# Products of one width together in the gate, up, B, C, x, q and k projections of a hybrid decoder layer

## The chip, the cores and the metric

The kernel runs on one core of one Trainium2 chip. The metric is the device time of one execution in microseconds; the time before is the median of three runs. A profile is one further execution, recorded by the hardware profiler. TensorE (PE) does the matmuls, ScalarE (ACT) and VectorE (DVE) do elementwise work, GpSimd (POOL) and SyncE (SP) mostly start transfers.

## The reference, cut to what matters

One decoder layer on 256 tokens of 1024 channels, all in float32: a gated feed-forward, a mixer with two branches in parallel, and a second gated feed-forward.

```python
h = h + 0.5 * rmsnorm(swiglu(rmsnorm(h, ffn1_pre_g), w_gate, w_up, w_down), ffn1_post_g)
u = rmsnorm(h, mix_pre_g)
z, xbc, dt_raw, q, k, v, gate_logits = split(u @ w_in)
y_ssd = ssd_branch(z, xbc, dt_raw, ...)      # convolution over xbc = (x, B, C), chunked state space
y_att = diff_attn_branch(q, k, v, ...)       # differential attention
h = h + rmsnorm((g0 * y_ssd + g1 * y_att) @ w_out, mix_post_g)
h = h + 0.5 * rmsnorm(swiglu(...), ffn2_post_g)
```

The projections in question are `x @ w_gate` and `x @ w_up` (1024 by 2816 each, in both feed-forwards), and the parts of `u @ w_in` that make B, C, x, q and k.

## The kernel before, in words

Each float32 operand of a projection is split into two parts of the matmul's reduced type: hi is the rounded value, lo is what is left. A product is the sum of three: weight hi by activation hi, weight hi by activation lo, weight lo by activation hi. The activations u lie as [128, 4, 2, 256] tiles, hi beside lo, so that one matmul of 512 columns does both products with a weight's hi part ("wide"), and one of 256 columns does the product with its lo part ("narrow").

Weights come in chunks of 1 MB, loaded by SyncE into three raw buffers (`load_to`, L232). `split_steps` (L244) makes hi by a ScalarE cast (whi, L259) and lo by a VectorE subtraction (wlo, L260), each in two halves. `take` (L306) keeps three chunks split ahead.

`mm_w` (L335) is one call: a chunk of 1024 by 256 weights, so two blocks of 128 outputs (half 0 and half 1). Each half has a PSUM bank of 512 columns. Half 0 does its 8 wide products and then its 8 narrow ones; half 1 does 8 narrow and then 8 wide. Each half is evicted when it is done: ScalarE copies the right 256 columns of the bank (L348, or L351 with a scale), and VectorE adds the left 256 to them (L349, L352). Both halves' banks come from `pj` (L81), a pool of three banks in turn. Another pool of five banks, `bg` (L89), serves transposes, scores and other background products.

Who calls it: the feed-forward loop (`ffn`, L881 to L898), gate and then up for each of nine chunks; C and B (L1203 to L1209, named pbc); x (L1489 to L1495, pxs); q and k in turn (L1510 to L1518, pq and pk), with a scale for q. Between x and q stands z (L1498 to L1504, pz), whose products are all narrow (`mm_t`) and whose bank ScalarE copies out (sz, L1503).

Beside these projections runs background work that Python generators hand out in steps (`Background`, L1461): each `back.run(us)` adds to what is due, and steps are emitted until their stated costs have used it up. During x it is `cb_work` (L1214): C times B for each group (pcb). During z, q and k it is `ssd_work` (L1227): transposes of x (px, L1233), the decay tiles E (made from a broadcast load acb by ScalarE and VectorE, L1249 to L1255; named by group, half and pair, such as E211), and the products py of E and X (L1265). Then `ssd_norm` (L1276, pn). In the attention and gates stage it is `att_work`.

Between L830 and L1523, so for most of both feed-forwards' gate and up calls and from C and B to the last k, the order of instructions on each engine is not the program's: the framework's scheduler places them by dependencies, priority and its own costs when the kernel is built. Each engine then runs its own list in that order. Elsewhere TensorE follows the program (`own_order`). The SiLU of z and its two changes of the activation table (L1505 to L1508) stand between z and q.

Of the kernel before, what the change touches and what calls it, by code (L numbers as in the profile page):

```python
# [18 lines left out]
AF = mybir.ActivationFunctionType  # L19
ALU = mybir.AluOpType  # L20
# [6 lines left out]
P = 128  # L27
T = 256
D = 1024
FF = 2816  # L30
KD = D // P
# [23 lines left out]
def tile_hybrid_layer(ctx: ExitStack, tc: tile.TileContext, x, ffn1_pre_g, ffn1_w_gate, ffn1_w_up,  # L55
# [4 lines left out]
    nc = tc.nc  # L60
# [5 lines left out]
    def k4(shape, name, dt=F32):  # L66
        return sb.tile(shape, dt, tag="k4", name=name, bufs=K4_BUFS)
# [4 lines left out]
    def k2(shape, name, dt=F32):  # L72
        return sb.tile(shape, dt, tag="k2", name=name, bufs=K2_BUFS)
# [7 lines left out]
    def pj(name):  # L81

        return ps.tile([P, 512], F32, tag="pj", name=name, bufs=3)
# [5 lines left out]
    def bg(shape, name):  # L89
        return ps.tile(shape, F32, tag="bg", name=name, bufs=5)  # L90
# [197 lines left out]
    def split_to(n):  # L288

        while len(splits) < min(n, len(units)):  # L290
            of, p = units[len(splits)]
            if p is not None:
                splits.append(of.split(p))
                continue
            for _ in split_steps():
                pass

    def ahead_of(i, n):

        n *= 4  # L300
        while n > 0 and i < len(units):
            n -= 4 if units[i][1] is None else 1
            i += 1
        return i

    def take(ahead=AHEAD):  # L306

        i = taken[0]
        taken[0] += 1
        split_to(ahead_of(i, ahead))  # L310
        (of, p), w = units[i], splits[i]
        splits[i] = None
        if p is not None:
            return w
        his, los = w
        nj = chunks[of][1][1] // 2
        return (lambda j: his[j // nj][:, j % nj, :], lambda j: los[j // nj][:, j % nj, :])
# [14 lines left out]
            for j in ks:  # L332
                nc.tensor.matmul(acc[m], wl(j)[:, cs], ah(k0 + j), start=False, stop=last and j == ks[-1])

    def mm_w(dst, name, w, act, scale=None):  # L335


        (wh, wl), (ah, _, ahl) = w, act
        for m in range(2):
            acc = pj(f"{name}{m}")  # L340
            cs = slice(m * P, (m + 1) * P)
            hi = [(acc, wh(j), ahl(j)) for j in range(KD)]
            lo = [(acc[:, :T], wl(j), ah(j)) for j in range(KD)]
            terms = lo + hi if m else hi + lo
            for i, (to, w_, x_) in enumerate(terms):
                nc.tensor.matmul(to, w_[:, cs], x_, start=i == 0, stop=i == len(terms) - 1, skip_group_check=m == 1)  # L346
            if scale is None:
                nc.scalar.copy(dst[:, m, :], acc[:, T:])  # L348
                nc.vector.tensor_tensor(dst[:, m, :], acc[:, :T], dst[:, m, :], ALU.add)  # L349
            else:  # L350
                nc.scalar.activation(dst[:, m, :], acc[:, T:], AF.Copy, scale=scale)  # L351
                nc.vector.scalar_tensor_tensor(dst[:, m, :], acc[:, :T], scale, dst[:, m, :], ALU.mult, ALU.add)  # L352

    def mm_nat(acc, w, act, k0, first, last, late):

# [32 lines left out]
    def act_table(name):  # L388
        f = nc.scalar.preload_act_table_set(name)
        for prev in act_since:  # L390
            tc.add_manual_dep(f.ins, prev, order, reason="activation table")
        act_since.clear()
        act_fence[0] = f.ins.name

    def act(*args, **kw):
        a = nc.scalar.activation(*args, **kw)
        if act_fence[0] is not None:
            tc.add_manual_dep(a.ins, act_fence[0], order, reason="activation table")
        act_since.append(a.ins.name)
        act_last[0] = a.ins  # L400
# [65 lines left out]
    for name, v in (("mx", mix_pre_g), ("f2", ffn2_pre_g),  # L466
                    ("ng", ssd_norm_g), ("cb", ssd_conv_b), ("sg", da_subln_g)):
        n = v.shape[1] // P
# [7 lines left out]
    def new_u(tag):  # L476
        for i in range(2):
            uT[i] = sb.tile([P, 4, 2, T], F32R, tag="u8", name=f"u{i}_{tag}", bufs=2)

    act_u = (lambda j: uT[j // 4][:, j % 4, 0, :], lambda j: uT[j // 4][:, j % 4, 1, :],  # L480
             lambda j: uT[j // 4][:, j % 4, :, :])
# [146 lines left out]
    def load_gain(v, name):  # L628
        pg = k4([P, D], name)
        nc.gpsimd.dma_start(pg, v[0].partition_broadcast(P))  # L630
        return pg
# [220 lines left out]
    def ffn(post_v, tag, ready, turned, then, products):  # L852
        gu = []

        gh = k4([P, 4, T], f"gh_{tag}0", F32R)
        gl = k4([P, 4, T], f"gl_{tag}0", F32R)
        gu += [(gh[:, m, :], gl[:, m, :]) for m in range(4)]
        sgs = []

        def evict(b, i, acc, r):  # L860
            if i == 0:
                sgs.append(k2([P, 512], f"sg_{tag}b{b}"))
                act(sgs[b], acc, AF.Silu, scale=1.0 if r is None else r)
            elif r is None:
                nc.vector.tensor_tensor(sgs[b], acc, sgs[b], ALU.mult)
            else:
                nc.vector.scalar_tensor_tensor(sgs[b], acc, r, sgs[b], ALU.mult, ALU.mult)

        def back(b):
            bs = slice(b * P, (b + 1) * P)  # L870
            pt_ = bg([P, 4, P], f"pt_{tag}{b}")
            for m in range(4):
                nc.tensor.transpose(pt_[:, m, :], sgs[b][:, m * P:(m + 1) * P], ident)
            split(gh[:, :, bs], gl[:, :, bs], pt_)

        products(evict, back)
        back(1)
        del sgs
        then()
        sums = {}  # L880
        for j in range(2, FF // T):  # L881
            if j % 2 == 0:
                gh = k4([P, 4, T], f"gh_{tag}{j}", F32R)
                gl = k4([P, 4, T], f"gl_{tag}{j}", F32R)
            o = (j % 2) * 2
            gu += [(gh[:, o + m, :], gl[:, o + m, :]) for m in range(2)]
            sg = k2([P, 2, T], f"sg_{tag}{j}")
            mm_w(sg, f"pg_{tag}{j}", take(), act_u)
            act(sg, sg, AF.Silu)
            su = k2([P, 2, T], f"su_{tag}{j}")  # L890
            mm_w(su, f"pup_{tag}{j}", take(), act_u)
            nc.vector.tensor_tensor(sg, su, sg, ALU.mult)  # L892
            split(gh[:, o:o + 2, :], gl[:, o:o + 2, :], sg)
            if j // 2 in QUADS[tag]:
                if j % 2:
                    sums[j // 2] = sums_of(j // 2, even, sg)
                else:
                    even = sg  # L898
        act_table(EXP_LN)
        acc, rest, combine, pairs = mm_quads(gu, sums, tag)  # L900
        pg = load_gain(post_v, f"pg_{tag}")

        norms = [{}, {}]

        quarters = (slice(0, 256), slice(256, 512)) if tag == "f2" else ()
        tail = [pj(f"tail{i}")[:, :256] for i in range(len(quarters))]

        def half(b, q):
            parts = quarters if b == 1 and q == 1 and quarters else (slice(0, 512),)
            r = rest[b][q]  # L910
            for cs in parts:
                behind(nc.vector.tensor_tensor(r[:, cs], acc[b][q][:, cs], r[:, cs], ALU.add), "lo")
            if len(parts) > 1:
                norm_quarters(norms[b], b, q, r, pg, 4.0, tag, parts, tail)
            else:
                norm_half(norms[b], b, q, r, pg, 4.0, tag)

        def done(b):
            norm_end(norms[b], b, 4.0, tag)
            ready(b)  # L920

        mm_n(acc, gu, done, turned, pairs=pairs, begin=False,
             taken_all=combine, norms=norms, half=half, quarters=quarters, tail=tail)
# [199 lines left out]
    for jj in range(2):  # L1123
        for a in (uh, ul):
            for i in range(4):
                k = i * 2 + jj
                nc.tensor.matmul(pdt[i * H_SSD:(i + 1) * H_SSD, :], wdt[:, k, :], a(k).bitcast(F32),
                                 start=jj == 0 and a is uh, stop=jj == 1 and a is ul)
# [73 lines left out]
    cT = k4([P, 4, T], "cT")  # L1202
    for i in range(4):  # L1203
        acc = k2([P, 2, T], f"bc{i}")
        mm_w(acc, f"pbc{i}", take(), act_u)
        dst = (bT, cT)[i // 2]
        conv(acc, 16 + 2 * i, dst[:, (i % 2) * 2:(i % 2) * 2 + 2, :])
        if i == 1:
            cumulated()  # L1209
# [108 lines left out]
    qT = [None] * 2  # L1318
    kT = [None] * 2
# [167 lines left out]
    back = Background()  # L1487
    back.add(cb_work())
    for g in range(4):  # L1489
        xs[g] = k4([P, 4, T], f"xs{g}")  # L1490
        for i in range(2):
            acc = k2([P, 2, T], f"xr{g}{i}")
            mm_w(acc, f"pxs{g}{i}", take(), act_u)
            conv(acc, g * 4 + i * 2, xs[g][:, i * 2:i * 2 + 2, :])
            back.run(0.4)  # L1495
    act_table(EXP_LN)
    back.add(ssd_work(range(4)))
    for g in range(4):  # L1498
        sz[g] = k4([P, 4, T], f"sz{g}")
        for i in range(2):  # L1500
            acc = pjt(f"pz{g}{i}")
# [8 lines left out]
    for c in range(4):  # L1510
        if c % 2 == 0:
            qT[c // 2] = k4([P, 4, T], f"q{c}")
            kT[c // 2] = k4([P, 4, T], f"k{c}")
        o = (c % 2) * 2
        mm_w(qT[c // 2][:, o:o + 2, :], f"pq{c}", take(), act_u, 0.125)
        back.run(QK_US)
        mm_w(kT[c // 2][:, o:o + 2, :], f"pk{c}", take(), act_u)
        back.run(QK_US)  # L1518

    back.add(att_work())  # L1520
# [80 lines left out]
    acc = [[bg([P, 512], f"acc_mx{b}{q}") for q in range(2)] for b in range(2)]  # L1601
# [50 lines left out]
```

## Time and profile before

| | |
|---|---|
| median of 3 runs | 730.47 us (730.29 to 732.0) |
| the profiled execution, and its span in the trace | 730.56 us, 728.9 us |
| granted TensorE clock, mean | 0.999 of full speed |
| DVE busy | 607.5 us, 83% of the span |
| first q to the end of the last k | 339.08 to 390.95 us |
| PE, DVE, ACT busy in that stretch | 51.87, 44.94, 39.10 us |

A row of the timeline has the start in microseconds from the span's start, the time the row covers, the engine, the line, the operation, the tile written and those read (buffer numbers left out), the shapes and the count. In brackets stands the idle time just before it, and what ended it. Matmuls overlap in the pipeline, so the spacing of starts is their cost, and a single one lasts longer than its spacing.

### The profile page before, as it was taken

The numbers are of one execution on the slowest core, as the hardware profiler recorded it, in microseconds if no ns is written. First come the engines' busy times: TensorE is split into PE (matmuls) and PEld (weight loads), VectorE is DVE, ScalarE is ACT, GpSimd is POOL, SyncE is SP. The second block draws the span as 40 slices with busy tenths as digits, with TensorE's granted clock in tenths as the row PEclk, the third lists the DMA queues.
The fourth block names the chain that finished last, engine by engine and source line by source line (L and its number), as shares of the span: only waits on it lengthen the run. The fifth ranks groups of instructions, "written<-read, shape, count | busy, mean of one in ns | idle before, by whom it ended". The sixth has DMA issues, their size and how long they took to land.

```text
span 728.9 us, 10550 instructions
## 1 busy us (share of the span) xinstructions
PE 721.7 (99%) x4025; PEld 620.8 (85%) x4025; DVE 607.5 (83%) x933; ACT 472.8 (65%) x804; POOL 30.9 (4%) x63
## 2 busy tenths in 40 slices
PE   9999999999999999999999999999999999999996
PEld 8888888888878889999888788888888888888885
DVE  6978788999979999777996997785784878789996
ACT  5657566667767676869965577782663757566562
POOL 4300000000200000000000000000010000000000
PEclk9999999999999999999999999999999999999999
DMA  8874645567664557665564664465461654654551
GB/s 299 233 262 147 226 161 186 174 223 268 195 217 123 170 172 248 212 205 176 164 222 148 210 209 147 142 244 190 125 237 43 232 187 161 230 197 150 176 199 58
DMA packets 94450, 137.92 MB, mean 189 GB/s; under 512 B 2668, under 2 KB 68800, under 8 KB 94400
## 3 DMA queue, kind: packets, MB, share of 16 engines
q1 hardware_dynamic: 91728, 129.51, 53.6%
q0 software_dynamic: 2368, 7.22, 3.3%
q8 instruction: 31, 0.51, 0.3%
q10 hardware_dynamic: 304, 0.53, 0.2%
q14 instruction: 19, 0.16, 0.1%
HBM read 136.17 MB, written 1.08 MB: 188 GB/s over the span
## 4 chain that ended last, share of the span: by engine, by line
PE 99%; DVE 0%; DVEq 0%; ACT 0%; issue 0%; ACTq 0%
PE pg_f L346 14%; PE pup_f L346 14%; PE pxs L346 6%; PE pws L363 6%; PE pgt L363 6%; PE acc_f2p L736 5%; PE acc_f1p L736 5%; PE pbc L346 3%; PE pk L346 3%; PE pq L346 3%; PE pn_f L379 3%; PE acc_mx L657 3%; PE pn_mx L363 3%; PE pn_f L363 3%; PE pwd L363 3%; PE acc_f1p L657 2%
## 5 line engine op out<-in xcount | busy, mean ns | idle before, releaser
L260 DVE TENSOR_TENSOR wlo<-raw,whi 128x1024 fp32r<-128x1024 f32 x216 | 257.5, 1219 | 19.0 <-ACT whi L259 17.8
L259 ACT CAST whi<-raw 128x1024 fp32r<-128x1024 f32 x216 | 219.4, 1050 | 14.1 <-DMA raw<-in_w_in_dram 3.5
L346 PE MATMUL pg_f<-u_f,whi 128*128 128x512 f32 x288 | 72.4, 392 | 0.0
L346 PE MATMUL pup_f<-u_f,whi 128*128 128x512 f32 x288 | 71.6, 391 | 0.0
L346 PEld LDWEIGHTS pup_f<-u_f,whi 128*128 128x128 f32 x288 | 52.9, 188 | 10.2
L346 PEld LDWEIGHTS pg_f<-u_f,whi 128*128 128x128 f32 x288 | 52.8, 188 | 10.1
L130 ACT CAST wqh<-wt 128x1024 fp32r<-128x1024 f32 x24 | 25.3, 1054 | 22.0 <-DVE wt L122 21.9
L346 PEld LDWEIGHTS pup_f<-u_f,wlo 128*128 128x128 f32 x288 | 37.1, 191 | 1.9 <-issue 0.3
L346 PEld LDWEIGHTS pg_f<-u_f,wlo 128*128 128x128 f32 x288 | 36.9, 191 | 1.4
L346 PE MATMUL pup_f<-u_f,wlo 128*128 128x256 f32 x288 | 37.8, 283 | 0.0
L346 PE MATMUL pg_f<-u_f,wlo 128*128 128x256 f32 x288 | 37.3, 283 | 0.0
L348 ACT COPY su_f<-pup_f 128x256 f32<-128x256 f32 x36 | 13.3, 370 | 36.7 <-PE pup_f L346 36.7
L349 DVE TENSOR_TENSOR su_f<-pup_f,su_f 128x256 f32<-128x256 f32 x36 | 15.1, 420 | 24.6 <-ACT su_f L348 24.6
L363 PE MATMUL pgt<-whi,u_mx 128*128 128x512 f32 x128 | 33.1, 393 | 0.0
L346 PE MATMUL pxs<-u_mx,whi 128*128 128x512 f32 x128 | 31.8, 394 | 0.0
L330 PE MATMUL pz<-u_mx,whi 128*128 128x256 f32 x128 | 31.6, 284 | 0.0
L331 PE MATMUL pz<-u_mx,whi 128*128 128x256 f32 x128 | 31.5, 284 | 0.0
L136 DVE TENSOR_TENSOR wql<-wt,wqh 128x1024 fp32r<-128x1024 f32 x24 | 29.1, 1219 | 0.2
L363 PEld LDWEIGHTS pgt<-whi,u_mx 128*128 128x128 f32 x128 | 23.6, 188 | 5.3 <-issue 0.7
L346 PEld LDWEIGHTS pxs<-u_mx,whi 128*128 128x128 f32 x128 | 23.2, 188 | 4.3
L320 ACT CAST gh_f<-sg_f 128x512 fp32r<-128x512 f32 x18 | 11.2, 620 | 23.3 <-DVE sg_f L892 23.3
L136 DVE TENSOR_TENSOR wql<-raw,wqh 128x1024 fp32r<-128x1024 f32 x18 | 21.8, 1219 | 4.4 <-ACT wqh L130 4.4
(415 smaller groups left out, 1585.7 us busy)
## 6 DMA issues: line engine op xcount, KB each, us to landing
raw<-in_w_in_dram SPq DMA_DIRECT2D x40, 1024.0 KB, 5.2
raw<-in_ffn_w_down_dram SPq DMA_DIRECT2D x22, 1024.0 KB, 4.8
raw<-in_ffn_w_gate_dram SPq DMA_DIRECT2D x20, 1024.0 KB, 5.4
raw<-in_ffn_w_up_dram SPq DMA_DIRECT2D x20, 1024.0 KB, 5.2
raw<-in_ssd_w_branch_dram SPq DMA_DIRECT2D x8, 1024.0 KB, 5.0
acb<-acd POOLq DMA_DIRECT2D x8, 512.0 KB, 4.4
raw<-in_da_w_branch_dram SPq DMA_DIRECT2D x4, 1024.0 KB, 5.0
raw<-in_w_out_dram SPq DMA_DIRECT2D x4, 1024.0 KB, 5.1
```

The source lines that it names most:

```text
L130: nc.scalar.copy(hi, src)
L136: nc.vector.tensor_sub(lo, src, hi.bitcast(F32))
L259: last_cast[0] = behind(nc.scalar.copy(hi, r[:, js, :]), "cast").ins
L260: m = nc.vector.tensor_sub(lo, r[:, js, :], hi.bitcast(F32))
L330: nc.tensor.matmul(acc[m], wh(j)[:, cs], ah(k0 + j), start=first and j == ks[0], stop=False)
L331: nc.tensor.matmul(acc[m], wh(j)[:, cs], al(k0 + j), start=False, stop=False)
L346: nc.tensor.matmul(to, w_[:, cs], x_, start=i == 0, stop=i == len(terms) - 1, skip_group_check=m == 1)
L349: nc.vector.tensor_tensor(dst[:, m, :], acc[:, :T], dst[:, m, :], ALU.add)
L363: nc.tensor.matmul(acc, a(k0 + j), b(j), start=first and i == 0, stop=last and i == 11)
L379: nc.tensor.matmul(accs[b], x_(k0 + j), w_(j), start=first and j == 0 and w_ is wh and x_ is acts[b][0], stop=last and j == 3 and w_ is wl)
L657: nc.tensor.matmul(acc[b][q][:, cs] if to is None else to, x_[:, ts], w_(kt)[:, halves[q]][:, cs], start=to is not None and kt == 0 and x_ ...
L736: nc.tensor.matmul(bank[p], x_, w_, start=p not in begun, stop=last and p in (1, 5, 6, 7))
```

## The change

`mm_w` becomes `mm_runs`. A call takes the products of one width for both halves together: an even call (n = 0) does half 0 wide, half 1 wide, half 0 narrow, half 1 narrow; an odd call (n = 1) does both narrow parts and then both wide parts. Each half is evicted after its second part, with the same two instructions as before. An odd call takes its two banks from the pool of five, unless `wide` is False; q and k pass False and are all odd. Gate is even and up odd; the four calls of B and C and the two of each x group alternate. In x the background is run after the even call alone, so C times B stands between a call that ends narrow and one that begins narrow.

```diff
+    def mm_part(acc, w, act, m, part, first):
+        (wh, wl), (ah, _, ahl) = w, act
+        to, w_, x_ = (acc, wh, ahl) if part == "hi" else (acc[:, :T], wl, ah)
+        for j in range(KD):
+            nc.tensor.matmul(to, w_(j)[:, m * P:(m + 1) * P], x_(j), start=first and j == 0,
+                             stop=not first and j == KD - 1, skip_group_check=True)
+    PARTS = (("hi", "lo"), ("lo", "hi"))
+    def mm_runs(dst, name, w, act, n, wide=True, scale=None):
+        banks = [bg([P, 512], f"{name}{m}") if n % 2 and wide else pj(f"{name}{m}") for m in range(2)]
+        for part in PARTS[n % 2]:
+            for m, acc in enumerate(banks):
+                mm_part(acc, w, act, m, part, part == PARTS[n % 2][0])
+                if part == PARTS[n % 2][1]:
+                    taken_from(acc, dst[:, m, :], scale)
...
-            mm_w(sg, f"pg_{tag}{j}", take(), act_u)
+            mm_runs(sg, f"pg_{tag}{j}", take(), act_u, 0)
...
-            mm_w(su, f"pup_{tag}{j}", take(), act_u)
+            mm_runs(su, f"pup_{tag}{j}", take(), act_u, 1)
...
-        mm_w(acc, f"pbc{i}", take(), act_u)
+        mm_runs(acc, f"pbc{i}", take(), act_u, i)
...
-            mm_w(acc, f"pxs{g}{i}", take(), act_u)
+            mm_runs(acc, f"pxs{g}{i}", take(), act_u, i)
             conv(acc, g * 4 + i * 2, xs[g][:, i * 2:i * 2 + 2, :])
-            back.run(0.4)
+            if i == 0:
+                back.run(0.4)
...
-        mm_w(qT[c // 2][:, o:o + 2, :], f"pq{c}", take(), act_u, 0.125)
+        mm_runs(qT[c // 2][:, o:o + 2, :], f"pq{c}", take(), act_u, 1, False, 0.125)
         back.run(QK_US)
-        mm_w(kT[c // 2][:, o:o + 2, :], f"pk{c}", take(), act_u)
+        mm_runs(kT[c // 2][:, o:o + 2, :], f"pk{c}", take(), act_u, 1, False)
```

`taken_from(acc, dst, scale)` is the copy and the add of L347 to L352, unchanged.

More of the change, by code (lines that the diff above doesn't have):

```diff
@@ L333, in mm_t, with taken_from @@
                 nc.tensor.matmul(acc[m], wl(j)[:, cs], ah(k0 + j), start=False, stop=last and j == ks[-1])
-    def mm_w(dst, name, w, act, scale=None):
+    def mm_part(acc, w, act, m, part, first):
         (wh, wl), (ah, _, ahl) = w, act
[L339 to L352, printed above, removed]
+        to, w_, x_ = (acc, wh, ahl) if part == "hi" else (acc[:, :T], wl, ah)
+        for j in range(KD):
+            nc.tensor.matmul(to, w_(j)[:, m * P:(m + 1) * P], x_(j), start=first and j == 0,
+                             stop=not first and j == KD - 1, skip_group_check=True)
+    def taken_from(acc, dst, scale=None):
+        if scale is None:
+            nc.scalar.copy(dst, acc[:, T:])
+            nc.vector.tensor_tensor(dst, acc[:, :T], dst, ALU.add)
+        else:
+            nc.scalar.activation(dst, acc[:, T:], AF.Copy, scale=scale)
+            nc.vector.scalar_tensor_tensor(dst, acc[:, :T], scale, dst, ALU.mult, ALU.add)
+    PARTS = (("hi", "lo"), ("lo", "hi"))
[6 more added lines that the diff above has]
+                    taken_from(acc, dst[:, m, :], scale)
     def mm_nat(acc, w, act, k0, first, last, late):
```

## The prediction

> **What bounds the kernel now.** I read first the page's busy table and its chain, then TensorE's timeline in the stages that the change touches, then ScalarE's and VectorE's timelines beside it.
>
> ```profile
> PE 721.7 (99%) x4025; PEld 620.8 (85%) x4025; DVE 607.5 (83%) x933; ACT 472.8 (65%) x804; POOL 30.9 (4%) x63
> ...
> PE 99%; DVE 0%; DVEq 0%; ACT 0%; issue 0%; ACTq 0%
> ```
>
> TensorE is busy for 99% of the span and carries 99% of the chain that ended last. So a gain has to come out of the matmuls' own spacing, and any wait that the change puts in front of a matmul is paid in full: there is no slack to hide it.
>
> In the timeline below a row's first number is the start of its first matmul, so the difference of two starts is what a row costs. "whi" rows are wide (512 columns), "wlo" rows narrow (256).
>
> ```profile
> 103.72 1.98 PE L346 MATMUL pup_f<-u_f,whi 128*128 128x512 f32 x8
> 105.53 2.08 PE L346 MATMUL pup_f<-u_f,wlo 128*128 128x256 f32 x16
> 107.44 2.00 PE L346 MATMUL pup_f<-u_f,whi 128*128 128x512 f32 x8
> 109.28 1.98 PE L346 MATMUL pg_f<-u_f,whi 128*128 128x512 f32 x8
> 111.09 2.08 PE L346 MATMUL pg_f<-u_f,wlo 128*128 128x256 f32 x16
> ```
>
> Eight wide behind wide cost 1.81 us (103.72 to 105.53, and 109.28 to 111.09), 0.227 each; eight wide behind narrow cost 1.84 (107.44 to 109.28). Sixteen narrow cost 1.91, 0.12 each. So a step from narrow to wide costs 0.03 us, and that is all that the change can take out of a call.
>
> **The change, part by part.** I compared the order in which the build places each kernel's instructions on the engines (there are no times in it). The matmuls are the same 3864; their neighbours differ. Steps from narrow to wide: 63 before, 38 after. They fall by 10 in each gated feed-forward (nine pairs of calls, and one pair of down products that no longer stands inside a call), by 2 in B and C, by 4 in x; in q and k they rise by 1 in sum, because there the build doesn't keep the groups together (below). Returns from plain fp32 work (transposes, py, C times B) to wide: 41 before, 35 after; to narrow: 5 before, 9 after.
>
> ```profile
> 340.92 1.95 PE L346 MATMUL pq<-u_mx,wlo 128*128 128x256 f32 x15
> 342.80 2.82 PE L1265 MATMUL py<-E,X 128*64 128x256 f32 x32
> 345.55 0.39 PE L346 MATMUL pq<-u_mx,wlo 128*128 128x256 f32 x1
> 345.78 2.00 PE L346 MATMUL pq<-u_mx,whi 128*128 128x512 f32 x8
> 347.61 1.03 PE L1233 MATMUL px<-ident,xs 128*128 128x128 f32 x8
> 348.40 2.07 PE L346 MATMUL pk<-u_mx,whi 128*128 128x512 f32 x8
> 350.31 2.08 PE L346 MATMUL pk<-u_mx,wlo 128*128 128x256 f32 x16
> ...
> 354.07 1.98 PE L346 MATMUL pq<-u_mx,whi 128*128 128x512 f32 x8
> ...
> 364.15 2.82 PE L1265 MATMUL py<-E,X 128*64 128x256 f32 x32
> 366.90 1.43 PE L346 MATMUL pk<-u_mx,whi 128*128 128x512 f32 x5
> 368.16 2.00 PE L346 MATMUL pq<-u_mx,whi 128*128 128x512 f32 x8
> ```
>
> *Savings.* 25 steps fewer at 0.03, less up to 0.01 each (a fresh narrow run of 16 takes 1.91, where 16 steps of 0.12 make 1.92): 25 x 0.025 = 0.6 us, between 0.5 and 0.75. Wide behind fp32: five take 1.26 (366.90 to 368.16) for 1.13, so 0.13 more; narrow behind fp32: one takes 0.23 (345.55 to 345.78) for 0.12, so 0.11 more. 6 x 0.13 - 4 x 0.11 = 0.35. Together 0.95 us, of which 0.6 lie ahead of the first q. Nothing runs over them, since TensorE is the chain itself.
>
> [...]
>
> *Evictions and banks.* Before, half 0 of a call is done 16 matmuls ahead of the call's end; now 8. In the feed-forwards, C, B and x this hides: odd calls take two of the five other banks, so a bank is written again only a whole call (5.6 us) or more after its half is done. The split weights cover too: by the build's order a call that begins narrow needs its low parts 1.8 us sooner, but they stand ready, three chunks ahead. I put both at nothing; if the cover failed it would be a wait of at most an eviction, under 1 us, at the start of a feed-forward.
>
> q and k are another matter: all their calls take the three pj banks, and each call now takes two at its start. Half 1 of a call needs the bank of half 0 of the call ahead, which was done 1.8 + 0.96 = 2.8 us earlier (eight wide, eight narrow), where before it had 5.6. An eviction is a ScalarE copy and then a VectorE add, each in its queue's place.
>
> ```profile
> 333.52 0.59 ACT L1503 COPY sz<-pz 128x512 f32<-128x512 f32 x1 [0.34 <-PE pz L333]
> ...
> 339.28 0.59 ACT L1503 COPY sz<-pz 128x512 f32<-128x512 f32 x1
> 339.76 1.28 ACT L396 ACTIVATE E<-acb,acs 128x128 f32<-128x128 f32 x4
> ...
> 348.08 1.05 ACT L259 CAST whi<-raw 128x1024 fp32r<-128x1024 f32 x1
> 349.04 0.65 ACT L351 ACTIVATE q<-pq 128x256 f32<-128x256 f32 x2
> 349.57 2.00 ACT L259 CAST whi<-raw 128x1024 fp32r<-128x1024 f32 x2
> 351.47 0.37 ACT L348 COPY k<-pk 128x256 f32<-128x256 f32 x1
> ...
> 355.79 1.28 ACT L396 ACTIVATE E<-acb,acs 128x128 f32<-128x128 f32 x4
> 356.98 0.62 ACT L396 ACTIVATE E<-E 128x512 f32<-128x512 f32 x1
> 357.50 1.27 ACT L396 ACTIVATE E<-acb,acs 128x128 f32<-128x128 f32 x4
> ```
>
> ```profile
> 349.17 1.23 DVE L260 TENSOR_TENSOR wlo<-raw,whi 128x1024 fp32r<-128x1024 f32 x1
> 350.31 0.75 DVE L352 SCALAR_TENSOR_TENSOR q<-pq,q 128x256 f32<-128x256 f32 x2
> ```
>
> Today the first q's half 0 is copied at 349.04 and added at 350.31 to 350.7, some 8 us after its last product; half 1 of k starts after the first eight of the narrow row at 350.31, so at 351.27. It gets by with about half a microsecond.
>
> In the changed order ScalarE does this: copy of z30, E blocks 200, 201, 210, one weight cast, copy of z31, one cast, E211, table, four SiLU, table, two casts, then q. Before, E200 and most of E201 stood ahead of z30's copy, and three of four casts ahead of z31's. So ScalarE now waits for z30's products with work behind it. Step by step on the clock of before: z30's copy at 333.52 - 0.6 = 332.9; 0.48 for it (339.76 less 339.28, rounded), three E blocks at 1.71 (355.79 to 357.50), a cast at 0.95 (two in 349.57 to 351.47): z31's copy at 339.45. From there to q's copy it was 349.04 - 339.28 = 9.76, now two casts more, 11.66: 351.1. VectorE must first split the two chunks' halves, 1.14 each (349.17 to 350.31), the first from the cast's end at 350.15: they end at 352.45, and the add of q's half 0 at 352.85.
>
> TensorE: first q at 339.08 - 0.6 = 338.48 (339.08 is 340.92 less eight wide behind narrow); 16 narrow 1.92, 15 wide 3.43, py 2.83, one wide 0.33, px 0.79, k's eight narrow 1.07, its eight wide 1.84: 350.7. Here it waits for the bank until 352.85: **2.15 us**. Eight narrow and eight wide more: k ends at 355.65 (354.07 before).
>
> Next, k's half 1 is copied right behind half 0 in ScalarE's queue, so ScalarE idles until 355.8; behind it are queued a cast, three E blocks, a cast and the copy of the second q: 0.3 + 0.95 + 5.13 + 0.95 puts that cast's end at 363.15, its VectorE split at 364.3, the add at 364.65. TensorE: second q 5.6, eight narrow and eight wide of the second k, 364.05: it waits **0.65 us**. From the third q on ScalarE has room and the waits end. That the build puts five wide products into the second q between its narrow halves, not eight, fits a first k that ended late.
>
> [...]
>
> Sum: 2.8 - 0.95 = +1.85 us. The profiled execution took 730.56 us (span 728.9), the median of the runs is 730.47; the forecast is 730.47 + 1.85 = **732.3**. Bounds: the first wait is between 0 (ScalarE at its old time, 349.04, and the two casts elsewhere) and 3.5 (z31's copy a further E block late); the second between 0 and 1.5.
>
> **Rivals.** *1. No wait, only the savings.* For: no row of TensorE in q and k shows a wait today, and the first of the two margins was kept. Against: two casts and three E blocks move behind a copy that waits for products. It would give 729.5.
> *2. Slower by more.* One mechanism: ScalarE reaches the first q's copy later than 351.1, because E200, E201 and E210 wait for their acb loads or VectorE halves behind z30's copy; each 0.1 us there is 0.1 us of TensorE. From 351.5 on the kernel is slower by over 0.3%; one E block late (1.5 to 1.7) gives 733.9. For: E blocks do wait for VectorE today. Against: their loads are issued well ahead in the new order.
> *3. A step of width costs nothing by itself.* The 0.03 us would belong to something beside it; the savings of 0.6 vanish, the waits stay: 732.9. Against it stand the rows, the same each time. [...]
>
> **How the numbers follow.** Forecast 0.57, own range 731.4 to 733.0; rival 1 0.14; rival 2 0.22; rival 3 0.07. 0.3%, about what a measurement here can tell from no change, is 2.2 us: under 728.3 is faster, over 732.66 slower. Slower: 0.07 of the forecast's share, rival 2, most of rival 3: 0.35. Faster: the far end of rival 1, 0.02. Same: 0.63. Range 729.5 to 733.9; 1 in 10 lies beyond each end.
>
> **What would show it.** Right: feed-forward rows of 16 and 32, and a call pair 0.03 us shorter; x calls going narrow, C times B, narrow; an idle TensorE of about 2 us ahead of the first k's second narrow run, released by VectorE's q add, and one under 1 us in the second k; ScalarE idle before z30's copy and before k's second copy. Wrong: q and k without a wait (rival 1), the first q's copy after 352 (rival 2), or a pair of calls as long as before (rival 3). A wait in the feed-forwards or in x would break the claim that banks and weights are covered there.

## The result, and the profile after

The changed kernel takes 734.26 us (median of 6 runs, 733.4 to 734.61), the kernel before 730.57 beside it (6 runs, 730.29 to 732.0). The ratio is 1.0042, 95% interval 1.0031 to 1.0052: slower by 3.1 us, between 2.3 and 3.8 (the two medians differ by 3.69). The forecast was +1.85, to 732.3. On its base of 730.47 the measured ratio gives 733.5: inside the whole range of 729.5 to 733.9, but over the forecast's own 731.4 to 733.0. By the prediction's line at 0.3% it is slower, to which it gave 0.35, against 0.63 for no change. The profiled execution took 734.61 us with a span of 732.7, so 4.05 us more than the one of before. In a later set (e11 below) the ratio was 1.0063.

The busy table and the chain of the changed kernel's page:

```profile
PE 721.7 (98%) x4025; PEld 620.2 (85%) x4025; DVE 608.9 (83%) x933; ACT 471.3 (64%) x804; POOL 31.5 (4%) x63
...
PE 91%; ACT 3%; DVE 2%; DMA 2%; issue 1%; SPq 0%; DVEq 0%; ACTq 0%
```

TensorE is busy for as long as before, and the span is 3.9 us longer: what came is waiting. The chain no longer runs over TensorE alone. TensorE's waits in the same kernel (engine and line, who ended the wait; total us, times, longest):

```profile
PE pk L341 <- DVE q L351: 2.8, 2, 2.2
PE warm L467 <- DVE zeros L447: 1.1, 1, 1.1
PE pu_mx L512 <- DVE h L637: 0.7, 1, 0.7
PE pu_f L949 <- DMA h<-in_x_dram: 0.3, 1, 0.3
```

Before, the list has only the second line. The last line stands at the very start of the kernel, ahead of all that changed. TensorE's timeline where pk waits:

```profile
349.22 1.20 PE L341 MATMUL pk<-u_mx,wlo 128*128 128x256 f32 x8
350.25 2.00 PE L341 MATMUL pk<-u_mx,whi 128*128 128x512 f32 x8
354.44 1.22 PE L341 MATMUL pk<-u_mx,wlo 128*128 128x256 f32 x8 [2.19 <-DVE q L351]
...
363.88 2.00 PE L341 MATMUL pk<-u_mx,whi 128*128 128x512 f32 x8
366.53 1.22 PE L341 MATMUL pk<-u_mx,wlo 128*128 128x256 f32 x8 [0.65 <-DVE q L351]
```

The brackets leave out some of it, since a row's length reaches past the next start. By starts, eight wide behind narrow cost 1.84, so the first wait is 354.44 - 350.25 - 1.84 = 2.35 us, the second 366.53 - 363.88 - 1.84 = 0.81. ScalarE in the same stretch, with the copies that the prediction followed:

```profile
334.34 0.59 ACT L1515 COPY sz<-pz 128x512 f32<-128x512 f32 x1 [6.19 <-PE pz L333]
334.82 1.28 ACT L407 ACTIVATE E<-acb,acs 128x128 f32<-128x128 f32 x4
...
340.85 0.58 ACT L1515 COPY sz<-pz 128x512 f32<-128x512 f32 x1
...
352.51 0.64 ACT L350 ACTIVATE q<-pq 128x256 f32<-128x256 f32 x2
...
357.54 0.37 ACT L347 COPY k<-pk 128x256 f32<-128x256 f32 x1 [2.22 <-PE pk L341]
```

ScalarE stands for 6.19 us in front of z30's copy, with the E blocks queued behind it, and again for 2.22 in front of the copy of k's half 1. The work that it didn't do in the first gap is what makes the first q's copy late. VectorE comes after it:

```profile
351.69 2.36 DVE L260 TENSOR_TENSOR wlo<-raw,whi 128x1024 fp32r<-128x1024 f32 x2
353.97 0.74 DVE L351 SCALAR_TENSOR_TENSOR q<-pq,q 128x256 f32<-128x256 f32 x2
```

Gate and up, against the rows of before:

```profile
98.11 3.79 PE L341 MATMUL pg_f<-u_f,whi 128*128 128x512 f32 x16
101.73 2.08 PE L341 MATMUL pg_f<-u_f,wlo 128*128 128x256 f32 x16
103.64 2.08 PE L341 MATMUL pup_f<-u_f,wlo 128*128 128x256 f32 x16
105.56 3.82 PE L341 MATMUL pup_f<-u_f,whi 128*128 128x512 f32 x16
109.22 3.56 PE L341 MATMUL pg_f<-u_f,whi 128*128 128x512 f32 x15
```

Rows of 16 stand in place of 8, and no wait is among them. A pair of calls takes 109.22 - 98.11 = 11.11 us, where two of before take 2 x 5.56 = 11.12; over all 18 pairs the steps of gate and up sum to 200.39 us against 200.78, so 0.02 less a pair.

Where the 3.86 us went, from the starts of the same products in the two timelines of TensorE (after less before):

| stretch | us |
|---|---|
| start, until the first gate product | +0.05 |
| first feed-forward | -0.16 |
| its end: pu_mx and the last products wait for h | +1.14 |
| C and B | -0.03 |
| x | -0.21 |
| z | +0.03 |
| q and k | +3.35 (waits 2.35 and 0.81, the rest 0.19) |
| gates, attention, mixing | +0.01 |
| second feed-forward | -0.32 |

### The profile page after: what moved, and what is told of

Same layout as the page of the kernel before. It is cut to its first block, busy times and chain, and to the rows that moved or that the text cites. A ratio compares the mean times of both kernels' runs of the same rounds, so it can differ in the third digit from the quotient of the medians.

```text
span 732.7 us, 10563 instructions
## 1 busy us (share of the span) xinstructions
PE 721.7 (98%) x4025; PEld 620.2 (85%) x4025; DVE 608.9 (83%) x933; ACT 471.3 (64%) x804; POOL 31.5 (4%) x63
## 4 chain that ended last, share of the span: by engine, by line
PE 91%; ACT 3%; DVE 2%; DMA 2%; issue 1%; SPq 0%; DVEq 0%; ACTq 0%
PE pup_f L341 14%; PE pg_f L341 14%; PE pxs L341 6%; PE pws L374 6%; PE pgt L374 6%; PE acc_f2p L747 5%; PE acc_f1p L747 5%; PE pbc L341 3%; PE acc_mx L668 3%; PE pn_mx L374 3%; PE pn_f L374 3%; PE pwd L374 3%; PE pn_f L390 2%; PE pk L341 2%; PE acc_f2p L668 2%; PE pz L331 2%
## 5 line engine op out<-in xcount | busy, mean ns | idle before, releaser
L341 PE MATMUL pg_f<-u_f,whi 128*128 128x512 f32 x288 | 69.0, 390 | 0.0
L341 PE MATMUL pup_f<-u_f,whi 128*128 128x512 f32 x288 | 68.7, 391 | 0.0
L347 ACT COPY su_f<-pup_f 128x256 f32<-128x256 f32 x36 | 13.2, 372 | 36.0 <-PE pup_f L341 36.0
L341 PE MATMUL pxs<-u_mx,whi 128*128 128x512 f32 x128 | 29.9, 390 | 0.0
```

The source lines that it names most:

```text
L341: nc.tensor.matmul(to, w_(j)[:, m * P:(m + 1) * P], x_(j), start=first and j == 0, stop=not first and j == KD - 1, skip_group_check=True)
```

## The experiments

**Theory O (order).** The second background call of each x group left the background's balance at 0; without it the balance is -0.4 us when z begins (four steps stated at 0.5 us each, against four additions of 0.4). That moves the E blocks and py by a call, the build puts z30's and z31's copies ahead of them on ScalarE, and the first q's copy comes late, whatever form q and k have. **Rival S (start).** The waits come from q and k taking two of the three banks at a call's start. Four kernels, run together on one chip with the kernel before, part the two.

*e1: the changed kernel, q and k in the old form.*

```diff
...
-mm_runs(qT[c // 2][:, o:o + 2, :], f"pq{c}", take(), act_u, 1, False, 0.125)
+mm_w(qT[c // 2][:, o:o + 2, :], f"pq{c}", take(), act_u, 0.125)
-mm_runs(kT[c // 2][:, o:o + 2, :], f"pk{c}", take(), act_u, 1, False)
+mm_w(kT[c // 2][:, o:o + 2, :], f"pk{c}", take(), act_u)
```

The dots stand for `mm_w` of the kernel before, put back beside `mm_runs`.

> The changed kernel, with q and k alone put back to the form of before (half 0 wide then narrow, half 1 narrow then wide); x keeps its one background call per group. Theory O (order): the two bank waits of the changed kernel, 2.35 and 0.81 us more than a wide step's own 0.227 at 351.87 and 365.49, come from ScalarE's order, which the background call dropped behind the second x call shifts; the first q's copy comes late whatever the form of q and k. By the build, ScalarE's order here is that of the changed kernel. So the waits stay, 2 to 3.2 us in sum, and the time is 733.0 to 734.5. Rival S (start): the waits come from a call taking two banks at its start; here it doesn't, so TensorE waits for nothing in q and k and the time is 730.2 to 731.3 (savings of about 0.5 us in the other stages, and up to 1.1 us of the wait for h at the end of the first feed-forward, if that belongs to the change).

734.93 us, ratio 1.0047 (1.0035 to 1.006): 0.4 over the range expected with the waits. Three of its six runs have a mean granted clock of 0.995, of which e5 and e11 say more. TensorE in e1:

```profile
348.68 2.09 PE L376 MATMUL pk<-u_mx,whi 128*128 128x512 f32 x8
350.61 1.11 PE L376 MATMUL pk<-u_mx,wlo 128*128 128x256 f32 x8
353.87 1.22 PE L376 MATMUL pk<-u_mx,wlo 128*128 128x256 f32 x8 [2.16 <-DVE q L382]
```

Half 1 of the first k begins 3.26 us behind eight narrow products that cost 0.96: a wait of 2.3 us, with the old form. The second is 0.86. Rival S falls.

*e2: the changed kernel, the background run after both x calls.*

```diff
-            if i == 0:
-                back.run(0.4)
+            back.run(0.4)
```

> The changed kernel, with the background call behind both x calls of a group, as before; q and k keep the changed form. Theory O (order): ScalarE's order from z to k is again that of before, nearly; the first q's copy is at its old place and TensorE's waits in q and k fall to under 0.5 us in sum: 730.3 to 731.4. Rival S (start): q and k still take two banks at a call's start, so the waits stay at 2 to 3.2 us and the time is 733.0 to 734.5. The second background call also puts C times B between two calls again, with two more returns from fp32 to a call in each x group: under 0.5 us.

730.58 us, ratio 0.999 (0.9982 to 0.9999). The list of TensorE's waits has no pk. ScalarE in e2, beside the same copies of before in the prediction (333.52, 339.28, 349.04):

```profile
333.53 0.59 ACT L1514 COPY sz<-pz 128x512 f32<-128x512 f32 x1 [0.34 <-PE pz L333]
...
339.29 0.59 ACT L1514 COPY sz<-pz 128x512 f32<-128x512 f32 x1
...
349.04 0.65 ACT L350 ACTIVATE q<-pq 128x256 f32<-128x256 f32 x2
```

q and k have the changed form here and wait for nothing.

*e3: the changed kernel, k's banks from the pool of five.*

```diff
-mm_runs(kT[c // 2][:, o:o + 2, :], f"pk{c}", take(), act_u, 1, False)
+mm_runs(kT[c // 2][:, o:o + 2, :], f"pk{c}", take(), act_u, 1)
```

> The changed kernel, with k's two banks from the pool of five, q's still from the three. ScalarE's order is that of the changed kernel up to the third k. If the bank is the place at which the late ScalarE reaches TensorE (theories O and S alike), k's half 1 needs no bank of q's half 0, and both waits go: 730.3 to 731.5. If ScalarE's lateness reaches TensorE elsewhere as soon as the bank lets go (E blocks for py, or the split weights of the next chunks, rival L), one wait takes the place of the other and the time stays over 732.5.

730.49 us, ratio 0.9989 (0.9981 to 0.9998), no pk in the list of waits. ScalarE in e3:

```profile
333.31 0.59 ACT L1515 COPY sz<-pz 128x512 f32<-128x512 f32 x1 [6.19 <-PE pz L333]
...
351.49 0.64 ACT L350 ACTIVATE q<-pq 128x256 f32<-128x256 f32 x2
```

ScalarE idles for the same 6.19 us and copies the first q 12.62 us behind its start (338.87), as late as in the changed kernel. So the late ScalarE reaches TensorE only through q's bank; with other banks it costs nothing.

*e4: the kernel before, q and k alone in the changed form.*

```diff
...
-mm_w(qT[c // 2][:, o:o + 2, :], f"pq{c}", take(), act_u, 0.125)
+mm_runs(qT[c // 2][:, o:o + 2, :], f"pq{c}", take(), act_u, 1, False, 0.125)
-mm_w(kT[c // 2][:, o:o + 2, :], f"pk{c}", take(), act_u)
+mm_runs(kT[c // 2][:, o:o + 2, :], f"pk{c}", take(), act_u, 1, False)
```

> The kernel before, with q and k alone in the changed form; everything ahead of them as before. Theory O: ScalarE's order is that of before up to the first q, the waits are under 0.5 us in sum and the time is 730.3 to 731.2. Rival S: 2 to 3 us of waits, 732.5 to 733.8. For the wait for h at the end of the first feed-forward (1.1 us more in the profiled run of the changed kernel, behind a cast that waited for a transfer): if it belongs to the changed gate and up, it is in the other three kernels of this set and not in this one; if the transfer was late by chance, it comes and goes without regard to that.

The dots stand for `mm_runs` and its helpers, added beside `mm_w`. 731.5 us, ratio 1.0001 (0.9993 to 1.001; before had 731.34 in this set), 0.3 over the expected 731.2. q and k take 0.01 us more than before, so their form is worth nothing either way. Its first feed-forward, in the old form, ends in a wait for h too, 0.42 us: that wait comes without the change.

The next four kernels shared another chip.

*e5: the kernel before, with the balance set by hand.*

```diff
+    back.due = -0.4
     act_table(EXP_LN)
     back.add(ssd_work(range(4)))
```

> The kernel before with one line more: the background's balance is set to -0.4 us ahead of the first z product, where before it stands at 0 and in the changed kernel at -0.4. No matmul of a projection changes its form, x keeps two background calls. Theory O: this balance alone sets ScalarE's order from z to k (by the build it is that of the changed kernel), so both bank waits are there, 2.3 and 0.8 us, and the time is 733.0 to 734.5. Rival: the waits of the changed kernel need something else of it (the place of C times B in x, or a call's two banks); then it is 730.2 to 731.5.

736.59 us, ratio 1.0065 (1.0052 to 1.0079), 2.1 over the range. One number, with no product changed, brings the waits. TensorE in e5:

```profile
351.86 1.11 PE L346 MATMUL pk<-u_mx,wlo 128*128 128x256 f32 x8
355.12 1.46 PE L346 MATMUL pk<-u_mx,wlo 128*128 128x256 f32 x8 [2.16 <-DVE q L352]
356.38 3.36 PE L346 MATMUL pk<-u_mx,whi 128*128 128x512 f32 x8
359.58 1.78 PE L346 MATMUL pq<-u_mx,whi 128*128 128x512 f32 x7
```

The first wait is 2.3 us again (355.12 - 351.86 - 0.96). Behind it eight wide products take 3.20 us instead of 1.84. Busy times by stretch of the same kernel, with the granted clock (each row: the stretch, its length, the busy times of PE, PEld, DVE, ACT and POOL with their counts, the granted clock, the DMA share, GB/s):

```profile
354.00:356.00 2.00, 0.88 (x7) 0.88 (x8) 2.00 (x5) 2.00 (x3) 0.00 (x0) 0.98 0.14 11
356.00:358.00 2.00, 2.00 (x7) 1.70 (x7) 2.00 (x3) 0.00 (x0) 0.00 (x0) 0.50 0.89 262
358.00:360.00 2.00, 2.00 (x7) 1.55 (x6) 1.59 (x4) 0.22 (x1) 0.00 (x0) 0.67 0.79 256
360.00:362.00 2.00, 2.00 (x12) 1.70 (x12) 1.68 (x4) 2.00 (x6) 0.00 (x0) 1.00 0.93 242
```

The clock was halved for some 3.4 us. That costs 1.36 for the wide row and 0.20 for the narrow one ahead of it (1.26, where the changed kernel's took 1.06). With a wait for h of about 1.1 us at the end of its first feed-forward, in the old form, this is why the profiled execution (737.16) lies over the range. The other four have no profile; two of them took 735.5 at a mean clock of 0.998 and 0.999, so over the range with no sign of a halved clock.

*e6: the changed kernel, the balance set back.*

```diff
+    back.due = 0.0
     act_table(EXP_LN)
     back.add(ssd_work(range(4)))
```

> The changed kernel with one line more: the balance is set to 0 ahead of the first z product, as it stands before; x keeps one background call per group. Theory O: no bank wait in q and k, and the savings of the other stages stay (0.17 us in the first feed-forward, 0.03 in B and C, 0.21 in x, 0.32 in the second feed-forward by the profiles so far; nothing in q and k): 0.7 us under the kernel before, 729.6 to 730.3 on a chip where before is 730.5. Rival: 733 or more, if C times B's place in x matters.

730.93 us, ratio 0.9992 (0.9984 to 1.0001; before had 730.98 in this set), 0.6 over the expected 730.3; no pk in the list. The waits are gone with x as the change has it. In all thirteen profiles of this document, z31's copy on ScalarE begins 0.95 us behind the first q in the six whose balance is -0.4, and 0.20 behind it in the seven where it is 0. By TensorE's starts the other stages keep their savings; that it is faster than before isn't clear of the interval.

*e7: e6, with q beginning wide from the three banks and k narrow from the five.*

```diff
-mm_runs(qT[c // 2][:, o:o + 2, :], f"pq{c}", take(), act_u, 1, False, 0.125)
+mm_runs(qT[c // 2][:, o:o + 2, :], f"pq{c}", take(), act_u, 0, scale=0.125)
-mm_runs(kT[c // 2][:, o:o + 2, :], f"pk{c}", take(), act_u, 1, False)
+mm_runs(kT[c // 2][:, o:o + 2, :], f"pk{c}", take(), act_u, 1)
```

> The same with q in the form that begins wide, from the three banks, and k beginning narrow from the five, so q and k alternate like gate and up. Candidate for the best: the groups now stay together, two or three steps from narrow to wide fewer than with one line reset alone, 0.1 us, if no E block or bank is late: 729.5 to 730.2. If the build's changed order of the second k behind part of the third q makes E or a bank late, 0.3 us or more slower than the reset alone.

730.06 us, ratio 0.9986 (0.9977 to 0.9995): the fastest here, though not clear of e2 and e3; 1.0 us under before by the ratio. By stretches it saves 0.17 in the first feed-forward, 0.03, 0.21 in x, 0.11 in q and k and 0.32 in the second feed-forward, and loses 0.06 in z: 0.78 in sum.

*e8: the kernel before, each half of gate and up wide, narrow, wide, narrow.*

```diff
+            if name.startswith(("pg_f", "pup_f")):
+                terms = [t for pair in zip(hi, lo) for t in pair]
...
```

> The kernel before with each half of the gate and up calls (36 calls in all) done wide, narrow, wide, narrow and so on, instead of eight and eight. The products are the same. Steps from narrow to wide rise from 1 inside a call to 16 with the border, 15 x 36 = 540 more, and as many from wide to narrow. If each step to wide costs 0.03 us and each to narrow gives 0.007 back (the profile of before), the time rises by 540 x 0.023 = 12 us, to 743. If only the first matmul behind a step is dearer or cheaper (233 instead of 227 ns, 113 instead of 120), it is about nothing: 730 to 731.5. If a step costs nothing by itself (rival 3 of the prediction): the same, 730 to 731.5, and the first wide step is 227 ns.

732.01 us, ratio 1.0007 (0.9998 to 1.0016), 0.5 over the range for a step that costs about nothing. The steps of gate and up sum to 202.01 us against 200.78 before: 1.23 for 540 steps, not 12. It isn't even in the two places: a wide matmul takes 237 ns in the first feed-forward and 231 in the second. Why they differ stays open.

A third set, on a third chip, asked how ScalarE's and VectorE's work turns into the wait, and what a step of width costs.

*e9: the changed kernel without two of four SiLU (two groups of z then go on without it, so this kernel computes something else).*

```diff
-    for g in range(4):
+    for g in range(2):
         act(sz[g], sz[g], AF.Silu)
```

> The changed kernel without the SiLU of the last two groups of z (z passes unchanged there, so two of the four groups are computed otherwise). This takes 1.95 us of ScalarE's work (two of four in 3.90) and one product of 1.14 us on VectorE from between z's copies and the first q's copy and add; the build keeps the order of TensorE up to the third q. If the queues of ScalarE and VectorE set the first bank wait, one for one: VectorE starts its split at 350.33 instead of 351.69, so the wait of the first k falls by 1.36, from 2.35 to 1.0 us, the second stays near 0.8, and the time is 1.4 us under the changed kernel of the same set. If the wait has another source (the bank's own order, a transfer), it stays at 2.3 and the time is that of the changed kernel.

733.18 us, ratio 1.0022 (1.0013 to 1.0032). Against the changed kernel of the same set (e11) the medians differ by 3.2 us, not the 1.4 expected, since halved clocks are likely in e11's (below) and e9's ten runs show no mean clock under 0.997; the profiled executions differ the other way (734.15 against 733.77), by the kernel's start and the wait for h. So the time is no test of the expectation, and the waits are. TensorE in e9:

```profile
350.67 2.00 PE L341 MATMUL pk<-u_mx,whi 128*128 128x512 f32 x8
353.48 1.22 PE L341 MATMUL pk<-u_mx,wlo 128*128 128x256 f32 x8 [0.81 <-DVE q L351]
...
362.91 2.00 PE L341 MATMUL pk<-u_mx,whi 128*128 128x512 f32 x8
366.19 1.22 PE L341 MATMUL pk<-u_mx,wlo 128*128 128x256 f32 x8 [1.28 <-DVE q L351]
```

The first wait is 353.48 - 350.67 - 1.84 = 0.97, as forecast (1.0), so 1.38 less for 1.36 of work taken away: the queues turn into the wait one for one. The second was expected near 0.8 and is 366.19 - 362.91 - 1.84 = 1.44. VectorE's product for the third group, 1.14 us, moved behind the first q and stands ahead of the second q's add:

```profile
362.58 1.22 DVE L1290 TENSOR_TENSOR xs<-xs,sz 128x1024 f32<-128x1024 f32 x1
```

So TensorE came 1.38 earlier and got back 0.75: a part of the gain turned into the next wait.

*e10: the kernel before, each half of gate and up in fours.*

```diff
+            if name.startswith(("pg_f", "pup_f")):
+                terms = hi[:4] + lo[:4] + hi[4:] + lo[4:]
...
```

> The kernel before with each half of the gate and up calls done as four wide, four narrow, four wide, four narrow. Steps from narrow to wide rise by 3 a call, 108 in all. If a change of width costs what alternating showed (540 more cost 1.7 us in the first feed-forward and -0.3 in the second), the sum is 0.1 to 0.4 us. If each run of wide products pays for its first four or five matmuls (233, 236, 229, 232 ns against 227 in the profile of before, 22 ns in sum, less 7 for the first narrow), 108 x 0.015 = 1.6 us. Read from the steps of the profiled run, gate and up alone: 200.8 us before, 202.4 by the second reading, 200.9 to 201.2 by the first.

732.57 us in a single run; gate and up sum to 202.30 us, against 202.4 and 200.9 to 201.2 of the two readings. 1.52 us for 108 steps is 0.014 each. TensorE in e10:

```profile
104.36 1.09 PE L348 MATMUL pup_f<-u_f,whi 128*128 128x512 f32 x4
105.29 0.63 PE L348 MATMUL pup_f<-u_f,wlo 128*128 128x256 f32 x4
105.76 1.09 PE L348 MATMUL pup_f<-u_f,whi 128*128 128x512 f32 x4
```

Four wide cost 0.93 (105.29 - 104.36), 0.022 over four at 0.227; four narrow cost 0.47, 0.01 under four at 0.12. So most of the 0.03 that a run of eight pays falls on its first four, and a run of one pays less (e8: 237 and 231 ns a wide matmul against 227).

*e11: the changed kernel once more.*

> The changed kernel itself once more, in the set of the kernel with two SiLU fewer, for comparison. The two bank waits are there at 2.3 and 0.8 us. Two things are open and told apart by its profile: whether TensorE's clock halves behind the first wait, as with the balance alone (427 ns for a wide matmul during some 3.4 us, 1.5 us lost) or not, as in the first profile of the changed kernel; and whether the wait for h at the end of the first feed-forward, 0.85 us then, is there again (by chance of a transfer, it may be anything from 0 to 1.3). 733.3 to 736.

736.38 us (4 runs, 733.77 to 736.85; before had 731.54), ratio 1.0063 (1.0046 to 1.008), partly over the range. The profiled execution, 733.77, has the two waits at 2.34 and 0.81, no halved matmul, and 0.7 us of waiting for h. Two of the other three runs have a mean granted clock of 0.995 and took 736.34 and 736.43; half a clock for 3.4 us, as in e5, takes 0.0023 from the mean over 734 us, so from 0.997 to 0.995. These two were not profiled, so the halving is argued for them, and for the fourth (736.85 at 0.997) the mean decides nothing, since the profiles without a halved matmul lie between 0.997 and 0.999.

## Why the prediction came out as it did

*The two waits: right in place and size.* On the clock of the first q's start (338.48 forecast, 339.90 measured) z31's copy was forecast at +0.97 and came at +0.95, q's copy at +12.62 and came at +12.61, TensorE reached the bank at +12.22 and +12.19, and got it at +14.37 and +14.54. The sum was 2.8 us; measured 3.16. The forecast rests on ScalarE working its queue in order; the 6.19 us that it idles in front of z30's copy, with the E blocks queued behind it, agree with that. (The forecast's second wait is 364.65 - 364.05 = 0.60, not 0.65; the sum stays 2.75, so 2.8.) The narrow product behind each wait takes 0.22 instead of 0.12, which makes the rest of q's and k's +3.35.

*Their cause: wrong in one half.* The prediction led with "each call now takes two at its start" and gave ScalarE's order as what makes the add late. e1 and e5 wait as long with q and k in the old form, e2 and e4 don't wait with the new one. ScalarE's order alone does it, and e5 shows that the balance of -0.4 alone sets that order. That the change in x was the costly line was not said.

*The savings: 0.95 forecast, 0.72 found* (0.16, 0.03, 0.21 and 0.32, before z's 0.03). The term was "a step from narrow to wide costs 0.03 us": read off a run of eight, it isn't a price of the step (e8: 0.002, e10: 0.014). For groups of 8 turned into 16 it still gave the right order: 0.48 of about 0.5 in the two feed-forwards (0.39 by the gate and up products alone). That it came so near is in part luck, since the price of a step it rests on did not hold. In q and k the forms are worth nothing (e4), where the prediction had part of the fp32 returns.

Four wide behind narrow cost 0.93 us in e10, against 0.91 for four at 0.227: what stands ahead of a matmul shows in its cost, but little. Over gate and up the change saved 0.4 of 200.78 us.

*Banks and split weights elsewhere: right.* No matmul of gate, up, B, C or x waits.

*Not in the sum.* The wait for h, 1.14 us in the profiled execution, with the slower products right behind it. ScalarE's casts there waited for a transfer of w_in; ScalarE in the changed kernel, then in the kernel before:

```profile
177.95 2.00 ACT L259 CAST whi<-raw 128x1024 fp32r<-128x1024 f32 x2 [5.56 <-DMA raw<-in_w_in_dram]
```

```profile
175.82 2.00 ACT L259 CAST whi<-raw 128x1024 fp32r<-128x1024 f32 x2 [3.11 <-DMA raw<-in_w_in_dram]
```

The transfer was issued 0.3 us earlier than before and landed 2.1 later: 7.8 us behind its issue, against 5.3. It doesn't need the change: e4 and e5 show such a wait in the old form (0.42, about 1.1), e2 and e7 show none in the new. Of the thirteen profiles, the transfer took 5.3 to 5.6 us in three (before, e2, e7) and 6.7 to 8.0 in the ten others, among them e4, e5, e8 and e10, whose gate and up are not in the changed form; the profile of before happens to be one of the three. What delays the transfer is open. Nor does the sum have the halved clock of e5: the profiled execution of the change had none. Without the wait for h and the start's 0.05, the profiled execution is 3.86 - 1.19 = 2.67 us longer, and that of e11, worked out the same way, 2.67 too; against the forecast's 1.85 that is 0.36 more of waits, 0.23 less of savings, 0.19 behind the waits and 0.04 elsewhere.

*The rivals.* Rival 1 (no wait) is what e6 and e7 are, 729.5 forecast for it; they have ratios of 0.9992 and 0.9986, so 0.6 and 1.0 us under before. Rival 2's time, 733.9, is nearer to what came than the forecast's, but its condition did not hold: ScalarE was not later than forecast. Rival 3 is not what the runs show either: grouping does save.

## What to carry to other kernels

A call that hands out background work does two things: it places the steps, and it leaves a balance that shifts every later step; before such a call is dropped, work out what it leaves and look at the order of the engines that evict, not only of the one that multiplies. On a kernel whose TensorE never waits, read each engine's queue in order and carry it forward instruction by instruction: that gave the waits here to 0.2 us. A difference read off one size of group is the price of that group, not of each step between groups: here a step there and back cost 0.023 us with groups of eight, 0.014 with fours and 0.002 with single products.

## What the runs showed of the hardware

Behind a wait of 2.3 us on TensorE the granted clock fell to 0.50 in e5. By the stretches above (0.98, 0.50, 0.67) it fell at about 355.9, some 0.8 us behind the end of the wait at 355.12, and was back at about 359.3, 3.4 us later. Eight wide matmuls took 3.20 us there instead of 1.84. Behind waits of the same length in the profiles of the changed kernel (2.35), e1 (2.3) and e11 (2.34) the clock stayed at 1.00. So a wait of this length cost 2.3 us in three profiles and 3.9 in one (2.3 + 0.20 + 1.36). What decided which of the two came, the runs don't show.

Wide and narrow matmuls of the reduced type in single alternation (e8) cost little over groups of eight (before): 177.0 ns a matmul in the first feed-forward and 173.8 in the second, against 174.3 in both.
